# Splitting eight more pairs of products a third time, with the two partial results of one output block joined by DMA

## The chip, the cores and the metric

The kernel runs on one core of a Trainium2 chip. The metric is the device time of one execution in microseconds (us); lower is better. The core has TensorE (PE, matmuls), VectorE (DVE), ScalarE (ACT), GpSimd (POOL, here only an issuer of DMAs) and SyncE (SP, an issuer of DMAs), each with its own queue of instructions in order, and 16 DMA engines that serve the DMAs of all queues.

## The reference

A mixture of experts with soft routing: every token goes through all eight experts, weighted by its softmax.

```python
# x: 16 x 512 x 512, router_logits: 16 x 512 x 8, expert_weights: 8 x 512 x 2048, all float32
probs = softmax(router_logits)
for e in range(8):
    output += probs[:, :, e:e+1] * np.matmul(x, expert_weights[e])
```

It is one matmul of a left side of 8192 x 4096 (x times the probability of each expert, the experts side by side) with a right side of 4096 x 2048.

## The kernel before

**Outer level.** The matmul is cut with Winograd's form of Strassen's method: seven products in place of eight. The left side is cut into 16 row blocks q of 512 tokens, each into an even and an odd half of 256 tokens (`h = 2q` and `2q + 1`), and into experts 0 to 3 and 4 to 7. The weights are cut into four blocks B11, B12, B21, B22 of 2048 x 1024. For each q there are the products P1 (even rows, experts 0 to 3, with B11), P2 (even rows, experts 4 to 7, with B21), and P5, P6, P7, P4, P3 on sums of these, with weights that are sums of blocks (`T1 = B11 - B12`, `T2 = B22 + T1`, `T3 = B22 - B12`, `T4`). C11, the even rows and first half of the columns, is P1 + P2. P1 is also an addend of M1, from which other blocks of the output come, so its result is kept in DRAM (`kept`) in any case.

**Inner level.** Each product (`Product`) is again cut by the same method into seven inner products, the steps 1, 5, 6, 2, 7, 3, 4. A step is 8 matmuls of 128 x 128 by 128 x 512, so a product has 56. One step of one product is called a slot. The left operands (`Left`: z, its `s2`, its `i`) are made by VectorE, the weights' inner sums (`inner_sums`) too. After each step `post` evacuates PSUM: `post_alone` mostly on ScalarE, `post_on_base`, for a product that adds a base, mostly on VectorE.

**Third level.** In some stages (`thirds`) the inner products 1 and 5 of a pair of products are cut once more, with the pair's two row blocks as the row halves: `by_thirds` runs 14 groups of four matmuls of 256 columns in place of four steps of eight matmuls of 512 columns, with left sums from `Thirds.make` on VectorE and weights from `third_sums`.

**Stages.** A stage is a pair of products with 14 slots, 112 matmuls or, split, 136. The list `stages` is in order: 15 stages of P1 and P2 (numbers 0 to 14, of which q = 0 and 1 of P1 are done ahead of them without an inner level), then stage 15 (`k5`) with two P5, 16 with one P6, 17 to 30 with P6 and P5, 31 (`k7`) with P6 and P7, 32 to 46 with P4 and P7, 47 (`k3`) with P4 and P3, 48 to 54 with two P3, and 55 with the last P3. Before, stages 0 to 3 hold P1 in pairs, 4 to 9 a P2 and a P1, 10 to 14 P2 in pairs; stages 1 to 3 and 48 to 54 are split.

**Order of the work.** From the first stage on, each engine's instructions stay in the order in which the program makes them. `hooks` (`at(stage, slot, make)`) put loads and sums at a slot; VectorE's work goes through one queue (`later`, `slack`), which a clock in the program empties as time allows. Loads of x and of the probabilities start two stages ahead (`start_loads`), the left operands are made one stage ahead (`queue_lefts`). A block of x that was not read before is loaded and cast by a DMA of POOL (`xs`) and transposed by DMAs of SP, then stored for later uses. Outputs, `kept` and weights sums are stored by POOL's DMAs (`pool`), bases are fetched by SP's (`Base.fetch`), sums of weights are fetched again by ScalarE's (`fetch_w`). Pools bound what can be under way: 15 weight tiles w (1 MB each), 12 tiles h for results, 10 tiles for x and probabilities. `wedge` loads half of one block of B12 and of B22 and makes T3, T1 and T2 of it.

**What P1 and P2 do with each other.** For q of 9 to 14 the P2 of a stage adds the P1 result of the stage before, which is still on chip; for the others it fetches `kept` as a base:

```python
if q >= QK:
    base = products[1, q].o.__getitem__
else:
    base = bases[2, q] = Base(kept_rows(q))
p = Product(right[2], left, to_out(q, 0, 0), base)
```

Of the kernel before, what the change touches and what calls it, by code (L numbers as in the profile page):

```python
# [31 lines left out]
def kernel(  # L32
# [19 lines left out]
    NB = 512  # L52
    NH = EH // 2
    WARM = 10
    HQ = 256
# [50 lines left out]
    def tt(o, a, b, op):  # L106
        dve(nc.vector.tensor_tensor(out=o, in0=a, in1=b, op=op))  # L107
# [12 lines left out]
    def pool(o, i, **how):  # L120
        note(nc.gpsimd.dma_start(out=o, in_=i, **how))  # L121
# [257 lines left out]
    def later(cost, make, first=False):  # L379
        t = Task(cost, make)  # L380
        (queue.appendleft if first else queue.append)(t)
        return t
# [238 lines left out]
                tt(o[tn], q if p in (5, 3) else x, base, ADD)  # L621


    QK = 9
    KEPT_Z = 14
    ND = QK // 2

    def out_rows(q, odd, cols, tn):
        t, n = tn
# [2 lines left out]
    def to_out(q, odd, cols, **how):  # L632
        return lambda tn, o: pool(out_rows(q, odd, cols, tn), o, **how)
# [59 lines left out]
    def kept_rows(q):  # L693
        return lambda tn: kept[q][tn[1], ds(tn[0] * HP, HP), :]

    def product(r, q, **how):
        left, loads = left_of(r, q)
        lefts[r, q] = left
        p = None
        if r == 1:  # L700
            def sink(tn, o):
                pool(kept_rows(q)(tn), o)
            p = Product(right[1], left, sink)
        elif r == 2:
# [24 lines left out]
        p.loads = loads  # L729
        products[r, q] = p  # L730
        return p

    products = {}
    forget = lambda *hs: [xs.pop(h, None) for h in hs]


    def start_loads(stage):
# [120 lines left out]
    forget(*range(0, 2 * QK, 2))  # L858
    rest = [15] + list(range(QK))
    for i in range(0, QK + 1, 2):  # L860
        k = add(product(2, rest[i]), product(2, rest[i + 1]))
        for slot, tn in zip((8, 10, 12, 13), INNER):
            for q in rest[i:i + 2]:
                if q < QK:
                    fetch_at(k if tn == (1, 0) else k - 1, 3 if tn == (1, 0) else slot, bases[2, q], tn)
    xs.clear()
    k5 = add(product(5, 0), product(5, 1))
    add(product(6, 0))
# [37 lines left out]
    def wedge(kn, e):  # L906

        t = new_w()
        a, b = t[:, ds(0, C), :], t[:, ds(C, C), :]
        rows = ds(e * C, C)  # L910

        def casts():
            cast_w(12, kn, e, a)
            cast_w(22, kn, e, b)

        def send(what, u):
            pool(kept_w(what, kn)[:, rows, :], u)

        def t3():
            u = new_u().rearrange("p (c two) t -> p c (two t)", two=2)  # L920
            tt(u, b, a, SUB)
            send("t3", u)

        def t1():
            tt(a, b11[kn][:, rows, :], a, SUB)
            send("t1", a)

        def t2():
            tt(b, b, a, ADD)
            send("t2", b)  # L930
        return casts, [t3, t1, t2]

    def wedge_at(stage, slot, kn, e, then):
        made = []

        def begin():
            casts, made_ = wedge(kn, e)
            casts()
            made.extend(made_)

        def go_on():
            for make in made:
                later(1.22, make)
        at(stage, slot, begin)
        at(*then, go_on)

    b21, t1, t2, t3 = {}, {}, {}, {}

    def cast21(kn):
        b21[kn] = cast_block(21, kn)  # L950

    for i, kn in enumerate(((0, 0), (0, 1), (1, 1), (1, 0))):
        at((11 * i + 8) // 14, (11 * i + 8) % 14, lambda kn=kn: cast21(kn))
# [12 lines left out]
    for i, (kn, e) in enumerate((kn, e) for kn in ((0, 0), (1, 0), (1, 1)) for e in range(2)):  # L966
        wedge_at(ND + i, 2, kn, e, (ND + i, 11))
# [4 lines left out]
    ODD = 0, 1  # L972


    made = {}

    def cast_odd(q):
        made[q] = cast_block(q, ODD)

    def odd_t():  # L980

        def make1():
            t1[ODD] = made[11]
            tt(t1[ODD], made[11], made[12], SUB)

        def make3():
            tt(made[12], made[22], made[12], SUB)
            pool(kept_w("t3", ODD), made.pop(12))

        def make2():  # L990
            t2[ODD] = made[22]
            tt(t2[ODD], made[22], t1[ODD], ADD)
        for make in (make1, make3, make2):
            later(2.29, make)

    def odd_t4():
        def make():
# [14 lines left out]
        return one(4, b[1, 0], b[1, 0], b[1, 1])  # L1012

    last2 = k5 - 1
    for stage, slot, q in ((9, 9, 12), (10, 2, 11), (10, 9, 22), (last2, 8, 21)):
        at(stage, slot, lambda q=q: cast_odd(q))
    at(11, 6, odd_t)
    for i, kn in enumerate(((0, 0), (1, 1), (1, 0))):
        fetch_at_w(11 + (8 + 4 * i) // 14, (8 + 4 * i) % 14, t1, "t1", kn)
        fetch_at_w(last2, 2 + 2 * i, t2, "t2", kn)  # L1020
    sums_at(12, 8, 5, t1, (5, 6))
    sums_at(13, 2, 5, t1, (7, 4))
    sums_at(last2, 9, 6, t2, (5, 6))
    at(k5, 4, odd_t4)
    sums_at(k5, 5, 6, t2, (7, 4))
# [10 lines left out]
    def part_of(what, kn, chunks):  # L1036
        return kept_w(what, kn)[:, chunks, :]
# [27 lines left out]
    def cast_part(q):  # L1065
        def load(t, kn, j, chunks):
            k, n = kn
            pool(t, expert_weights[(q // 10 - 1) * HE + 2 * k + j // 2, ds(j % 2 * 2 * P, 2 * P),
                                   ds((q % 10 - 1) * NH + n * NB, NB)].rearrange("(c p) n -> p c n", p=P))
        return load  # L1070

    def load_part(what):
        def load(t, kn, j, chunks):
            pool(t, part_of(what, kn, chunks))
        return load
# [7 lines left out]
            pool(part_of("t4", kn, chunks), t)  # L1083
        later(0.69, make)

    def keep_raw(t, kn, chunks):
        pool(part_of("b22", kn, chunks), t)

    by_parts(k5 + 2, 4, 13, 7, load_part("t3"), None, (7,))
    by_parts(*slots_after(k5 + 2, 4, 56), 28, 4, load_p4, less_t2, (9, 20))  # L1090
    by_parts(k7 + 4, 4, 36, 3, cast_part(22), keep_raw, (9, 16))


    RAW = {1: (0, 0), 2: (1, 0), 3: (1, 1)}
# [30 lines left out]
        return load.begin  # L1125
    at(k3 - 1, 10, load_z(0))
    at(k3, 2, load_z(1))
    third3 = {}

    def third_of_p3(p):  # L1130
        def make():
            third3[p] = third_sums(right[3].w[p])
        later(2.76, make)
    at(k3, 3, lambda: third_of_p3(1))
    at(k3, 5, lambda: third_of_p3(5))
    wait_for[k3] = 6


    finish = products[3, 15]
    finish.base = Base(lambda tn: out_rows(15, 0, 1, tn))  # L1140
# [79 lines left out]
```

## Time and profile before

| | before |
|---|---|
| median of 3 runs | 1369.01 us (1368.84 to 1369.75) |
| profiled execution, first to last instruction (span) | 1367.0 us |
| PE busy | 1359.6 us (99%) |
| DVE busy | 1124.8 us (82%) |
| ACT busy | 207.3 us (15%) |
| POOL busy | 411.8 us (30%) |
| moved by DMA | 360.09 MB |

The profiled execution is known by its span; the runs lie 1.8 to 2.8 us above it, the median 2.0 us, for what lies around the first and last instruction. The rows in the text below are from that one execution. A row of a group gives busy time, mean ns of one, then the engine's idle time ahead of them and what ended it; a row of the timeline gives start, length, engine, line and operation, and in brackets the idle time ahead. A matmul's end is modelled, so rates are taken from starts. A line can be that of a helper: L107 is every VectorE tensor operation, L121 every DMA of POOL, L130 every matmul.

### The profile page before, as it was taken

The numbers are of one execution on the slowest core, as the hardware profiler recorded it, in microseconds if no ns is written. First come the engines' busy times: TensorE is split into PE (matmuls) and PEld (weight loads), VectorE is DVE, ScalarE is ACT, GpSimd is POOL, SyncE is SP. The second block draws the span as 40 slices with busy tenths as digits, with TensorE's granted clock in tenths as the row PEclk, the third lists the DMA queues.
The fourth block names the chain that finished last, engine by engine and source line by source line (L and its number), as shares of the span: only waits on it lengthen the run. The fifth ranks groups of instructions, "written<-read, shape, count | busy, mean of one in ns | idle before, by whom it ended". The sixth has DMA issues, their size and how long they took to land.

```text
span 1367.0 us, 18181 instructions
## 1 busy us (share of the span) xinstructions
PE 1359.6 (99%) x6630; PEld 645.4 (47%) x6630; DVE 1124.8 (82%) x1358; ACT 207.3 (15%) x397; POOL 411.8 (30%) x652
## 2 busy tenths in 40 slices
PE   9999999999999999999999999999999999999999
PEld 4555444444444444444444444444444444556554
DVE  7868767679789888788887888888889898898884
ACT  3232111100011111111111100000000000223331
POOL 3233233331223343333322112232332422233232
PEclk9999999999999999999999999999999999999999
DMA  9999999999899999999999998888897979999876
GB/s 185 207 246 233 229 254 255 244 294 385 252 309 273 334 343 317 292 277 316 309 302 324 322 399 240 199 237 208 231 265 203 259 184 298 328 306 240 189 122 127
DMA packets 193290, 360.09 MB, mean 263 GB/s; under 512 B 53168, under 2 KB 87216, under 8 KB 187696
## 3 DMA queue, kind: packets, MB, share of 16 engines
q0 software_dynamic: 88688, 185.12, 56.8%
q1 hardware_dynamic: 100480, 145.36, 35.4%
q10 hardware_dynamic: 4032, 28.44, 5.3%
q8 instruction: 52, 0.85, 0.3%
q14 instruction: 38, 0.31, 0.1%
HBM read 214.99 MB, written 171.11 MB: 282 GB/s over the span
## 4 chain that ended last, share of the span: by engine, by line
PE 97%; DMA 3%; POOL 0%; issue 0%; ACT 0%; DVE 0%; ACTq 0%; POOLq 0%; DVEq 0%
PE ps L130 71%; PE pt L130 25%; DMA h<-out_dram 2%; DMA w<-wd 1%; DMA w<-in_expert_weights_dram 1%; POOL w L121 0%; ACT h L614 0%; DVE ps L107 0%; ACT h L1168 0%; ACTq L164 0%; POOL ident L225 0%; POOLq L225 0%; DVEq L107 0%; POOLq L1204 0%
## 5 line engine op out<-in xcount | busy, mean ns | idle before, releaser
L130 PE MATMUL ps<-w,z 128*128 128x512 f16 (+1 forms) x3704 | 812.2, 376 | 0.8 <-DMA w<-wd 0.5
L130 PEld LDWEIGHTS <-z 128*128 128x128 f16 x5336 | 522.0, 98 | 606.2 <-issue 1.7
L121 POOL DMA_DIRECT2D out_dram<-h x380 | 248.8, 679 | 729.4 <-ACT h L614 337.0
L130 PE MATMUL pt<-w,z 128*128 128x512 f16 (+1 forms) x1632 | 357.7, 369 | 0.6 <-DMA w<-in_expert_weights_dram 0.5
L107 DVE TENSOR_TENSOR h<-ps,h 128x512 f32<-128x512 f32 x260 | 176.8, 686 | 120.9 <-PE ps L130 112.3
L107 DVE TENSOR_TENSOR z<-xT,pT 128x2048 f16<-128x2048 f16 x220 | 266.4, 1216 | 8.2 <-issue 7.2
L130 PE MATMUL ps<-w,d 128*128 128x512 f16 x880 | 199.1, 379 | 0.0
L107 DVE TENSOR_TENSOR h<-pt,h 128x512 f32<-128x512 f32 x155 | 105.7, 687 | 53.5 <-PE pt L130 46.7
L130 PEld LDWEIGHTS <-d 128*128 128x128 f16 x880 | 86.1, 98 | 101.7
L107 DVE TENSOR_TENSOR z<-z,d 128x2048 f16<-128x2048 f16 x110 | 132.4, 1215 | 0.0
L107 DVE TENSOR_TENSOR w<-w 128x1024 f16<-128x1024 f16 (+2 forms) x108 | 111.1, 1039 | 3.4 <-DMA w<-wd 1.7
L614 ACT COPY h<-ps 128x512 f32<-128x512 f32 x64 | 37.5, 586 | 486.2 <-PE ps L130 415.5
L601 ACT COPY h<-ps 128x512 f32<-128x512 f32 x90 | 52.7, 585 | 372.4 <-PE ps L130 316.0
L107 DVE TENSOR_TENSOR d<-z 128x1024 f16<-128x1024 f16 x110 | 74.6, 683 | 0.9
L107 DVE TENSOR_TENSOR ps<-ps,h 128x512 f32<-128x512 f32 (+1 forms) x86 | 54.0, 628 | 22.7 <-PE ps L130 18.6
L121 POOL DMA_DIRECT2D wd<-w x86 | 48.3, 585 | 41.6 <-DVE w L107 26.2
L121 POOL DMA_DIRECT2D w<-in_expert_weights_dram x65 | 48.9, 784 | 38.0 <-DMA wd<-w 28.1
L121 POOL DMA_DIRECT2D kept<-h x56 | 30.8, 550 | 60.2 <-DVE h L107 27.3
L597 ACT COPY h<-ps 128x512 f32<-128x512 f32 x65 | 36.7, 598 | 76.8 <-PE ps L130 67.3
L107 DVE TENSOR_TENSOR h<-h 128x512 f32<-128x512 f32 (+2 forms) x69 | 45.0, 674 | 0.6 <-ACT h L601 0.5
L107 DVE TENSOR_TENSOR z<-z,u 128x2048 f16<-128x2048 f16 x36 | 44.1, 1225 | 1.2
L107 DVE TENSOR_TENSOR u<-xT,pT 128x2048 f16<-128x2048 f16 x36 | 43.8, 1216 | 0.0
(72 smaller groups left out, 352.5 us busy)
## 6 DMA issues: line engine op xcount, KB each, us to landing
out_dram<-h POOLq DMA_DIRECT2D x380, 256.0 KB, 6.9
pT<-p_dram SPq DMA_DIRECT2D x126, 256.0 KB, 6.8
w<-wd ACTq DMA_DIRECT2D x27, 1024.0 KB, 9.7
h<-kept SPq DMA_DIRECT2D x100, 256.0 KB, 7.4
xT<-x SPq DMA_DIRECT2D x73, 256.0 KB, 6.7
wd<-w POOLq DMA_DIRECT2D x72, 256.0 KB, 7.5
w<-in_expert_weights_dram POOLq DMA_DIRECT2D x35, 512.0 KB, 10.5
h<-out_dram SPq DMA_DIRECT2D x68, 256.0 KB, 5.3
```

The source lines that it names most:

```text
L107: dve(nc.vector.tensor_tensor(out=o, in0=a, in1=b, op=op))
L121: note(nc.gpsimd.dma_start(out=o, in_=i, **how))
L130: note(nc.tensor.matmul(ps, z, w, start=start, stop=stop, skip_group_check=True))
L597: act(nc.scalar.copy(o[tn], q if p == 5 else x))
L601: act(nc.scalar.copy(o[TN[p]], b if p == 2 else x))
L614: act(nc.scalar.copy(o[tn], b))
```

## The change

P1 gets stages 0 to 6 in pairs, P2 stages 7 to 14 in pairs. Stages 1 to 5 and 8 to 13 are split a third time, where 1 to 3 were. P2 writes its result to the output without a base, and later 64 DMAs of POOL (`add_kept`), from DRAM to DRAM, add P1's kept result to it, 256 KB each: four per stage in stages 10 to 13, then one every five or six slots from stage 32 to 46, and four each in stages 49 and 50. T1 is no longer stored and fetched but made in place of B11 (`in_place`), all four blocks go through `wedge` (the block (0, 1) in stages 2 and 4, the others in stages 7 to 12), B22 is kept from there for the last P3 weights, and T2 is fetched in four blocks in stage 14. The third-level weights of P2 (`third2`) are made in stage 7. The diff, cut to its core:

```diff
-    ND = QK // 2
+    ND = 7
...
-            if q >= QK:
-                base = products[1, q].o.__getitem__
-            else:
-                base = bases[2, q] = Base(kept_rows(q))
-            p = Product(right[2], left, to_out(q, 0, 0), base)
+            p = Product(right[2], left, to_out(q, 0, 0))
...
-    for q in range(2, QK, 2):
+    for q in range(2, 16, 2):
         add(product(1, q), product(1, q + 1))
-    for q in range(QK, 15):
-        add(product(2, q), product(1, q + 1))
...
+    for q in range(0, 16, 2):
+        add(product(2, q), product(2, q + 1))
...
+        own = b11[kn][:, rows, :]
...
-        def t1():
-            tt(a, b11[kn][:, rows, :], a, SUB)
-            send("t1", a)
+        def in_place():
+            tt(own, own, a, SUB)
         def t2():
-            tt(b, b, a, ADD)
-            send("t2", b)
+            send("b22", b)
+            tt(a, b, own, ADD)
+            send("t2", a)
...
+    for kn, where in zip(((0, 0), (0, 1), (1, 1), (1, 0)), ((1, 8), (3, 2), (5, 0), (5, 9))):
+        at(*where, lambda kn=kn: cast21(kn))
...
+    for i, (kn, e) in enumerate((kn, e) for kn in (ODD, (0, 0), (1, 1), (1, 0)) for e in range(2)):
+        stage = ND + i - 2 if kn != ODD else 2 + 2 * i
+        wedge_at(stage, 2, kn, e, (stage, 11))
...
+    for i, kn in enumerate(ORDER):
         fetch_at_w(last2, 2 + 2 * i, t2, "t2", kn)
...
-    by_parts(k7 + 4, 4, 36, 3, cast_part(22), keep_raw, (9, 16))
+    by_parts(k7 + 4, 4, 36, 3, load_part("b22"), None, (9,))
...
+    third_at(ND, 5, third2, 2, 1)
+    third_at(ND, 7, third2, 2, 5)
...
+    def add_kept(q, n, t):
+        pool(out_f[ds(2 * q * HQ + t * HP, HP), ds(n * NB, NB)], kept[q][n, ds(t * HP, HP), :], accum_op=ADD)
+
+    for q in range(16):
+        for i in range(4):
+            where = (ND + 3, 14 * q + 3 * i) if q < 4 else (k7 + 1, 21 * (q - 4) + 5 * i) if q < 14 else (k3 + 2, 14 * (q - 14) + 3 * i)
+            at(*slots_after(where[0], 0, where[1]), lambda q=q, i=i: add_kept(q, i // 2, i % 2))
...
-    for stage in range(1, ND):
+    for stage in range(1, ND - 1):
         thirds[stage] = Thirds(*(p.left for p in stages[stage]), third)
+    for stage in range(ND + 1, last2):
+        thirds[stage] = Thirds(*(p.left for p in stages[stage]), third2)
```

More of the change, by code (lines that the diff above doesn't have):

```diff
@@ L621, in post_on_base @@
                 tt(o[tn], q if p in (5, 3) else x, base, ADD)
-    QK = 9
     KEPT_Z = 14
-    ND = QK // 2
+    ND = 7
     def out_rows(q, odd, cols, tn):
@@ L733 @@
     products = {}
-    forget = lambda *hs: [xs.pop(h, None) for h in hs]
     def start_loads(stage):
@@ L851, in fetch_at @@
             at(stage, slot, lambda tn=tn: base.fetch(tn))
-    for q in range(2, QK, 2):
+    for q in range(2, 16, 2):
         add(product(1, q), product(1, q + 1))
-    for q in range(QK, 15):
-        add(product(2, q), product(1, q + 1))
[L858 to L865, printed above, removed]
+    xs.clear()
+    for q in range(0, 16, 2):
+        add(product(2, q), product(2, q + 1))
     xs.clear()
@@ L922, in t3 @@
             send("t3", u)
-        def t1():
-            tt(a, b11[kn][:, rows, :], a, SUB)
-            send("t1", a)
+        def in_place():
+            tt(own, own, a, SUB)
         def t2():
-            tt(b, b, a, ADD)
-            send("t2", b)
-        return casts, [t3, t1, t2]
+            send("b22", b)
+            tt(a, b, own, ADD)
+            send("t2", a)
+        return casts, [t3, in_place, t2]
     def wedge_at(stage, slot, kn, e, then):
@@ L945, in wedge_at @@
         at(*then, go_on)
-    b21, t1, t2, t3 = {}, {}, {}, {}
+    b21, t2 = {}, {}
     def cast21(kn):
         b21[kn] = cast_block(21, kn)
-    for i, kn in enumerate(((0, 0), (0, 1), (1, 1), (1, 0))):
-        at((11 * i + 8) // 14, (11 * i + 8) % 14, lambda kn=kn: cast21(kn))
+    for kn, where in zip(((0, 0), (0, 1), (1, 1), (1, 0)), ((1, 8), (3, 2), (5, 0), (5, 9))):
+        at(*where, lambda kn=kn: cast21(kn))
     def sums_at(stage, slot, r, of, ps):
@@ L965 @@
     sums_at(ND - 1, 12, 2, b21, (4,))
-    for i, (kn, e) in enumerate((kn, e) for kn in ((0, 0), (1, 0), (1, 1)) for e in range(2)):
-        wedge_at(ND + i, 2, kn, e, (ND + i, 11))
+    ODD = 0, 1
+    for i, (kn, e) in enumerate((kn, e) for kn in (ODD, (0, 0), (1, 1), (1, 0)) for e in range(2)):
+        stage = ND + i - 2 if kn != ODD else 2 + 2 * i
+        wedge_at(stage, 2, kn, e, (stage, 11))
     def fetch_at_w(stage, slot, of, what, kn):
@@ L971 @@
     ORDER = ((0, 0), (0, 1), (1, 1), (1, 0))
-    ODD = 0, 1
     made = {}
@@ L978, in cast_odd @@
         made[q] = cast_block(q, ODD)
[L980 to L994, printed above, removed]
     def odd_t4():
@@ L1014 @@
     last2 = k5 - 1
[L1015 to L1019, printed above, removed]
+    at(last2, 8, lambda: cast_odd(21))
+    for i, kn in enumerate(ORDER):
         fetch_at_w(last2, 2 + 2 * i, t2, "t2", kn)
-    sums_at(12, 8, 5, t1, (5, 6))
-    sums_at(13, 2, 5, t1, (7, 4))
+    for stage, slot, p in ((last2 - 2, 8, 5), (last2 - 1, 2, 6), (last2 - 1, 8, 7), (last2, 1, 4)):
+        sums_at(stage, slot, 5, b11, (p,))
     sums_at(last2, 9, 6, t2, (5, 6))
@@ L1084, in less_t2 @@
         later(0.69, make)
-    def keep_raw(t, kn, chunks):
-        pool(part_of("b22", kn, chunks), t)
     by_parts(k5 + 2, 4, 13, 7, load_part("t3"), None, (7,))
     by_parts(*slots_after(k5 + 2, 4, 56), 28, 4, load_p4, less_t2, (9, 20))
-    by_parts(k7 + 4, 4, 36, 3, cast_part(22), keep_raw, (9, 16))
+    by_parts(k7 + 4, 4, 36, 3, load_part("b22"), None, (9,))
     RAW = {1: (0, 0), 2: (1, 0), 3: (1, 1)}
@@ L1127, with third_at @@
     at(k3, 2, load_z(1))
-    third3 = {}
-    def third_of_p3(p):
+    third2, third3 = {}, {}
+    def third_at(stage, slot, of, r, p):
         def make():
[L1132 to L1135, printed above, removed]
-    wait_for[k3] = 6
+            of[p] = third_sums(right[r].w[p])
+        at(stage, slot, lambda: later(2.76, make))
+    third_at(ND, 5, third2, 2, 1)
+    third_at(ND, 7, third2, 2, 5)
+    third_at(k3, 3, third3, 3, 1)
+    third_at(k3, 5, third3, 3, 5)
+    wait_for[k3] = 6
+    def add_kept(q, n, t):
[4 more added lines that the diff above has]
+            at(*slots_after(where[0], 0, where[1]), lambda q=q, i=i: add_kept(q, i // 2, i % 2))
     finish = products[3, 15]
```

## The prediction

> **What bounds the kernel now.** I read the page first (span, engines, clock, the chain that ended last), then busy time by stretches, with the stretches laid on stages, then TensorE's timeline at a stage's start, the DMA view of single stages, and last the chain of waits around the one place where TensorE stops.
>
> ```profile
> span 1367.0 us, 18181 instructions
> ...
> PE 1359.6 (99%) x6630; PEld 645.4 (47%) x6630; DVE 1124.8 (82%) x1358; ACT 207.3 (15%) x397; POOL 411.8 (30%) x652
> ...
> PEclk9999999999999999999999999999999999999999
> DMA  9999999999899999999999998888897979999876
> ...
> PE 97%; DMA 3%; POOL 0%; issue 0%; ACT 0%; DVE 0%; ACTq 0%; POOLq 0%; DVEq 0%
> ```
>
> TensorE carries 97% of the chain at the full clock, so time comes from the number of matmuls and from places where TensorE stops. VectorE is 82% busy and the DMA engines look full nearly everywhere: these two hand back what fewer matmuls gain. By stretches (stage bounds found by counting matmuls; x counts one neighbour too many on TensorE):
>
> ```profile
> core 0: us, PE busy (x) PEld busy (x) DVE busy (x) ACT busy (x) POOL busy (x), PEclk, DMA share, GB/s
> 200.00:600.00 400.00, 400.00 (x1855) 181.32 (x1853) 326.64 (x380) 47.24 (x81) 126.85 (x222) 1.00 1.02 299
> ...
> 64.48:87.94 23.46, 23.46 (x137) 13.30 (x136) 16.79 (x23) 8.46 (x18) 6.51 (x11) 1.00 1.26 239
> 87.94:111.32 23.38, 23.38 (x137) 13.31 (x136) 16.61 (x22) 8.40 (x18) 7.50 (x14) 1.00 1.21 225
> 255.57:279.74 24.17, 24.17 (x113) 10.98 (x112) 16.72 (x20) 3.50 (x6) 9.34 (x16) 1.00 1.10 250
> 799.47:824.78 25.31, 24.50 (x113) 10.87 (x112) 20.27 (x24) 1.17 (x2) 5.38 (x8) 1.00 1.04 389
> 824.78:848.95 24.17, 24.17 (x113) 10.95 (x112) 20.43 (x24) 1.17 (x2) 5.69 (x9) 1.00 0.87 237
> 1210.76:1234.40 23.64, 23.54 (x137) 13.29 (x136) 21.59 (x27) 8.23 (x18) 8.21 (x10) 1.00 1.07 275
> 1304.54:1327.92 23.38, 23.38 (x137) 13.31 (x136) 19.81 (x25) 8.23 (x18) 6.93 (x9) 1.00 0.69 90
> ```
>
> Stages of 112 matmuls take 24.17 us, split stages of 136 take 23.38 us (stages 2 and 53), and of the stages shown only stage 1 (+0.08), stage 32 (799.47, +1.14) and stage 49 (1210.76, +0.26) took longer. So a stage lasts as long as its matmuls, even at a DMA share of 1.26, until something is late by more than its lead.
>
> **The change, part by part.** A slot is one step of one product: 8 matmuls, 8 x 0.2157 = 1.73 us. *Eight more split pairs.* Before, stages 1 to 3 and 48 to 54 are split; after, stages 1 to 5 (P1), 8 to 13 (P2) and 48 to 54. The number of stages is the same. Each newly split pair swaps 32 matmuls of 512 columns for 56 of 256: 8 x 24 = 192 more matmuls, which the built program has. The split part of stage 1 begins and ends here:
>
> ```profile
> 64.48 1.04 PE L130 MATMUL pt<-w,z 128*128 128x256 f16 x8
> ...
> 70.59 1.67 PE L130 MATMUL ps<-w,d 128*128 128x512 f16 x7
> ```
>
> 56 matmuls in 70.59 - 64.48 = 6.11 us are 109.1 ns each. A 512-column one takes 400 / 1854 = 215.7 ns (one off for the edge). 32 x 215.7 = 6.90 us against 6.11 us is 0.79 us per pair, the same as 24.17 - 23.38. Eight pairs save **6.3 us**. [...]
>
> *VectorE's work.* The prices:
>
> ```profile
> L107 DVE TENSOR_TENSOR h<-z 128x1024 f16<-128x1024 f16 x6 | 4.1, 686 | 0.1
> L107 DVE TENSOR_TENSOR u<-w 128x2048 f16<-128x2048 f16 x6 | 7.3, 1215 | 0.0
> ```
>
> A split pair's own work is in the rows of stages 1 and 2: 16.6 to 16.8 us. P2 pairs become like P1 pairs, because they no longer add a base: their results are evacuated by ScalarE (8.4 us busy in a split stage, off the path). On top, stages 2, 4 and 7 to 12 each get a wedge (half of one of the four weight blocks: T3, T1 and T2 in three operations), 3 x 1.215 = 3.6 us. That makes 20.3 of 23.38 us; stage 49's row carries 21.59 and loses 0.26. The two blocks of third-level weights for P2 are 8 x 0.686 = 5.5 us in stage 7, not a split stage; its 27 operations, counted in the program, are 9 of 1.215 and 18 of 0.686 us, 23.3 of 24.17, and what is last in the queue is a wedge that nobody waits for. I take 0, with 0.3 per stage as the upper end.
>
> *Loads of P1 in pairs.* The pairs of stages 4 to 6 now need two raw x blocks each (before, one from stage 4 on), loaded two stages ahead by POOL's casting load and SP's transposes. Before, that was already close (the DMA view of 55 to 62 us, with the median time to land, and VectorE's timeline):
>
> ```profile
> xT<-xs SPq DMA_TRANSPOSE x4, 14.8
> ```
> ```profile
> 77.49 1.22 DVE L107 TENSOR_TENSOR z<-xT,pT 128x2048 f16<-128x2048 f16 x1 [4.44 <-issue]
> ...
> 83.75 0.68 DVE L107 TENSOR_TENSOR h<-ps,h 128x512 f32<-128x512 f32 x1
> ```
>
> Transposes issued there, beside B21's casting loads, took 14.8 us to land, and VectorE stood 4.44 us before a z (the row says "issue"; transposes issued up to 62 land up to 77, so I read them as the cause). The evacuation of step 7 then ran at 83.75 and ended at 84.43; the second product's step 4, whose bank it frees, starts about 2 x 1.73 us before the stage's end at 87.94, at 84.5. TensorE lost 0.08 us. So another 1 us of lateness is 1 us lost. After, the cast of one block starts at stage 1's slot 8 and two half blocks at the wedges in stages 2 and 4, so five stages come near this edge; bounds 0 and 5 x 1 us, and below 0 only the 0.08. I take 0.3, near the row, which got through.
>
> *What leaves the queues.* The fetches of P1's results into P2's bases go (36 from SP), T1's way through DRAM goes, and the last P3 weights are loaded and not cast. T2 is now fetched by ScalarE's queue in four blocks instead of three in stage 14, two slots apart, and the sum that needs the third is queued three slots (5.2 us) after it:
>
> ```profile
> w<-wd ACTq DMA_DIRECT2D x27, 1024.0 KB, 9.7
> ```
>
> So VectorE may stand 9.7 - 5.2 - 2.4 (the sum before it, 2 x 1.215) = 2.1 us there, and the evacuations behind it have two slots, 3.5 us: 0, with 1 as upper end.
>
> *The 64 added DMAs.* Each reads 256 KB of P1 from DRAM and adds it into 256 KB of the output. No such DMA is in the trace. The nearest are the accumulating stores of P3, alone in stage 53 (the DMA view of 1304.54 to 1327.92; columns packets, MB, share of 16 engines):
>
> ```profile
> q0 software_dynamic: 1150, 2.09, 68.7%
> ...
> out_dram<-h POOLq DMA_DIRECT2D x9, 256.0 KB, 6.8
> ```
>
> 0.687 x 23.38 = 16.1 us for eight of them (the ninth is cut by the edge): 2.0 us of all 16 engines each, 6.8 us to land. An addition from DRAM cannot write less than that, and its source read is one more DRAM access, so the upper bound is twice, 4 us. I take 2.0. In stages 10 to 13 four per stage (8 us) come where eight fetches went, at shares that row 255.57 shows to be harmless at 1.10. In stages 32 to 46 it is 2.7 per stage, 5.3 us or 0.22 of a stage: stage 33's 0.87 becomes 1.09, harmless by the same row. In stages 49 and 50, 1.07 becomes 1.41, beyond any row; but an output tile there is needed again seven slots (12 us) after its last store, against 6.8 to land: I take 0.2, upper end 3. Stage 32 is the place that pays. TensorE's timeline there, the chain of waits, and the DMA view of the stage:
>
> ```profile
> 821.32 7.08 PE L130 MATMUL ps<-w,z 128*128 128x512 f16 x32 [0.49 <-DMA w<-wd]
> ```
> ```profile
> 788.08 20.68 DMA h<-out_dram
> ...
> 809.26 12.02 DMA w<-wd
> ```
> ```profile
> q10 hardware_dynamic: 602, 4.31, 40.4%
> q1 hardware_dynamic: 1941, 3.53, 38.7%
> q0 software_dynamic: 693, 1.96, 24.2%
> ```
>
> A base fetch issued at 788.08 takes 20.7 us and the weights of P4's step 4 are issued behind it and take another 12.0 us; TensorE waits for them, the stage is 1.14 us long. The engines have no room here (sum 1.03 at 389 GB/s). After, additions start at slots 0 and 5 of this stage, before those weights land (a third at slot 10 comes behind them). Each adds up to 2.0 us in front of one link of that chain: bounds 0 (they fit into dips; not below, since nothing leaves this stage) and 4.0. I take 2.0, the middle, since no row is nearer to one end.
>
> **Sum.** -6.3 + 0.3 + 0.2 + 2.0 = -3.8 us. The span becomes 1367.0 - 3.8 = 1363.2; the median of the runs lies 2.0 us over the profiled span, so 1369.0 - 3.8 = **1365.2 us**.
>
> **The rivals.** (a) *The additions hide entirely*: stage 32's 1.14 us stays, nothing else appears, 1369.0 - 6.3 = 1362.7. For it: everywhere else a share over 1.0 cost nothing. Against: stage 32's chain has no lead left. 15%.
>
> (b) *P1's transposes come too late*, at the edge shown above: up to 1 us in each of five stages beyond the forecast, up to 1370.2, the middle 1367.7. For it: wedge casts now stand beside the transposes in stages 2 and 4. Against: two casts stood there in stages 0 to 2 too. 15%.
>
> (c) *Slower: POOL's queue blocks behind the additions.* In the built program every POOL DMA waits for the one eight before it. Stages 10 to 12 have 17 POOL DMAs each and 13 has 14, counted in the program: eight take at least 8 x 23.38 / 17 = 11.0 us. If an addition lands after more than that, the output stores behind it start late, and the 12 h tiles (a split stage without room of its own wants 14) come free late; ScalarE's copy of step 6 has four slots, 6.9 us, before step 7 needs its bank. The slowest 256 KB seen is the 20.7 us above: 20.7 - 11.0 - 6.9 = 2.8 us in each of four stages, 11.2 us, **1376.4**. It is slower than before by more than the bound from about (3.8 + 2.7) / 4 + 17.9 = 19.5 us of landing. For it, from the waits of ScalarE (total, times, longest):
>
> ```profile
> ACT h L601 <- DMA out_dram<-h: 56.4, 5, 17.3
> ```
>
> Output tiles do come free late at times. Against: accumulating stores land in 6.8 us. 18%.
>
> (d) *256 columns cost more than half of 512*, because a weight load no longer hides beside the shorter matmul:
>
> ```profile
> L130 PEld LDWEIGHTS <-z 128*128 128x128 f16 x5336 | 522.0, 98 | 606.2 <-issue 1.7
> ```
>
> From 6.90 / 56 = 123 ns per matmul on the split saves nothing. With a fifth of the 98 ns laid bare it would take 109 + 20 = 129 ns and cost 56 x 0.129 - 6.90 = 0.3 us per pair: 1369.0 + 2.6 + 2.5 = 1374.1. The rows say 109.1, all hidden. 1%. [...]
>
> (e) *The gain does not arrive*: the change does what it says, but the six P2 stages wait for VectorE as stage 49 does, 6 x 0.3 us, and stage 32 pays its upper end: -6.3 + 1.8 + 4.0 + 0.5 = 0, 1369.0. Against: the 20.3 us above are under stage 49's 21.59. 6%.
>
> **How the numbers follow.** The forecast has 45%. Its own spread is the bounds of stage 32: 1363.2 to 1367.2. This kernel's measurement tells about 0.2%, 2.7 us, from no change: the line lies at 1366.3. Faster: 15 from (a), 41 of the forecast's 45, 2 of (b) = 0.58. Same: 4 of the forecast, 12 of (b), 6 of (e) = 0.22. Slower: (c), (d) and 1 of (b) = 0.20. The range goes from just under (a), 1362.0 (half of stage 32's 1.14 gone too), over (b) and (e) to 1371.0, which is also the forecast with the additions' upper price (8.0 for stage 32 in place of 2.0, 1371.2); it leaves out (c) and (d).
>
> **What would show it.** Stages 4, 5 and 8 to 13 at 23.38 us each: the first term. Stage 32 at 26 to 29 us with its last matmuls waiting for w<-wd: the third. Additions landing in 7 to 10 us and a share of about 1.1 in stages 33 to 46: their price. Wrong would be: additions landing after 20 us, POOL waiting on its own DMAs in stages 10 to 13, a stage of 8 to 13 over 24.17 us, or VectorE standing more than 5 us before a z in stages 2 to 6.

## The result, and the profile after

The changed kernel takes 1373.82 us (median of 5 runs, 1372.35 to 1376.47) against 1369.01 us: 1.0038 times as long, interval 1.0026 to 1.0051. The forecast was 1365.2 us, with 1362.0 to 1371.0 as range. It is slower by 4.8 us, not faster by 3.8.

From the page of the changed kernel (span, busy time, DMA share by slices, POOL's queue, the chain that ended last, the added DMAs as a group of instructions, then as issues with their landing time):

```profile
span 1374.7 us, 18740 instructions
...
PE 1356.7 (99%) x6822; PEld 664.7 (48%) x6822; DVE 1125.2 (82%) x1369; ACT 263.5 (19%) x525; POOL 461.2 (34%) x707
...
DMA  9899997899999999999999999999998999999976
...
q0 software_dynamic: 93536, 199.80, 62.1%
...
PE 81%; DMA 15%; issue 2%; DVE 1%; POOL 1%; ACT 0%; DVEq 0%; POOLq 0%; ACTq 0%
...
L121 POOL DMA_DIRECT2D out_dram<-kept x64 | 61.4, 1002 | 17.9 <-DMA out_dram<-h 12.8
...
out_dram<-kept POOLq DMA_DIRECT2D x64, 256.0 KB, 9.7
```

VectorE's busy time is what it was, and TensorE's is 2.9 us less, yet the span is 7.7 us longer (1374.7 against 1367.0; this execution is the slowest of the five, so its losses are some 3 us larger than the median's). The chain says where to look: before, TensorE carried 97% of it, now 81%, and DMAs 15%. TensorE waits in a few places. By stretches, laid on the stages by counting matmuls (stages 4, 8, 6, 19, 20, 32, 33 and 51):

```profile
core 0: us, PE busy (x) PEld busy (x) DVE busy (x) ACT busy (x) POOL busy (x), PEclk, DMA share, GB/s
135.35:158.73 23.38, 23.38 (x137) 13.32 (x136) 15.96 (x21) 8.23 (x18) 7.98 (x14) 1.00 1.12 233
235.27:258.65 23.38, 23.38 (x137) 13.32 (x136) 18.51 (x24) 8.20 (x18) 7.54 (x14) 1.00 0.90 248
...
182.11:211.10 28.99, 26.02 (x113) 11.40 (x112) 18.50 (x16) 5.84 (x10) 4.32 (x8) 0.94 0.91 253
484.33:510.30 25.97, 24.34 (x113) 10.97 (x112) 19.10 (x25) 3.50 (x6) 9.07 (x17) 1.00 1.09 306
510.30:536.06 25.76, 24.33 (x113) 10.97 (x112) 21.46 (x29) 3.50 (x6) 10.36 (x20) 1.00 1.10 335
802.33:828.08 25.75, 24.51 (x114) 10.87 (x112) 20.52 (x24) 1.17 (x2) 8.10 (x11) 1.00 1.05 354
828.08:853.75 25.67, 24.34 (x114) 10.95 (x113) 20.09 (x24) 1.17 (x2) 7.73 (x12) 1.00 0.94 262
1262.31:1287.61 25.30, 23.70 (x137) 13.30 (x136) 20.64 (x26) 8.24 (x18) 10.92 (x14) 1.00 1.04 257
```

Against 24.17 (112 matmuls) and 23.38 (136), and against the same stages before, the account of this execution is:

| where | us |
|---|---|
| eight newly split stages (4, 5, 8 to 13), each exactly 23.38 | -6.3 |
| stage 6 | +4.8 |
| stages 19 and 20 | +3.4 |
| stages 31 to 33 (3.45 over; before 1.15) | +2.3 |
| stage 51 | +1.9 |
| stages 1 and 49 (0.08 and 0.26 over before, now 0) | -0.3 |
| last stage | +1.2 |
| ahead of the first stage | +0.7 |
| sum | +7.7 |

**Stage 6.** VectorE's timeline, then TensorE's, both of the changed kernel:

```profile
192.43 1.23 DVE L107 TENSOR_TENSOR z<-xT,pT 128x2048 f16<-128x2048 f16 x1 [10.56 <-DMA xT<-xs]
...
198.50 6.81 DVE L107 TENSOR_TENSOR w<-w 128x4096 f16<-128x4096 f16 x3
205.23 1.28 DVE L107 TENSOR_TENSOR h<-ps,h 128x512 f32<-128x512 f32 x2
```
```profile
199.38 3.62 PE L130 MATMUL pt<-w,z 128*128 128x512 f16 x16
205.96 6.38 PE L130 MATMUL ps<-w,z 128*128 128x512 f16 x21 [2.97 <-DVE h L107]
```

VectorE stands 10.56 us before a left operand of stage 7, the transposes of a raw x block not having landed. Behind it in the queue are the other left operands (6.1 us), then three weight sums of P2 (6.8 us), then the evacuation that TensorE needs: it runs at 205.23, and TensorE has stood 2.97 us. Why the transposes are late stands a stage earlier, in the DMA view of 155 to 168:

```profile
w<-in_expert_weights_dram POOLq DMA_DIRECT2D x2, 512.0 KB, 13.9
...
xs<-in_x_dram POOLq DMA_DIRECT2D x2, 256.0 KB, 15.6
```

Stage 7 is P2 of q = 0 and 1, whose x blocks no stage has read before (P1 of q = 0 and 1 is done ahead of them). So POOL loads two raw x blocks in stage 5, two stages ahead, right behind the casting loads of `cast21` at slot 0. The x blocks take 15.6 us to land, SP's transposes can only start then, at the end of the stage, and slot 9 puts another block of B21 beside them.

The other 1.85 us of stage 6 (28.99 - 24.17 - 2.97) are nearly all slow matmuls, and the PEclk column shows them: 0.94 over the stage. The 21 matmuls behind the stop take 6.38 us; at full speed 21 take 20 x 0.2157 + 0.38 (the length of the last) = 4.69 us, 1.69 less. The remaining 0.16 is how a stop is counted, from the modelled end of the matmul ahead of it.

**Stage 51.** The chain of waits ahead of it and the DMA view of stages 49 and 50 (1215.5 to 1262.3), where the last eight additions were put:

```profile
1220.44 18.93 DMA out_dram<-kept
1239.37 20.17 DMA out_dram<-h
...
1260.56 17.70 DMA out_dram<-h
...
1278.35 0.60 ACT h L597
```
```profile
out_dram<-h POOLq DMA_DIRECT2D x13, 256.0 KB, 19.1
out_dram<-kept POOLq DMA_DIRECT2D x7, 256.0 KB, 19.4
```

Before, the stores of the same two stages (the DMA view of 1210.8 to 1258):

```profile
out_dram<-h POOLq DMA_DIRECT2D x18, 256.0 KB, 7.9
```

All accumulating stores land in 19 us there, where they took 7.9 before (6.8 alone in stage 53). The DMA share of the two stages hardly rose, to 1.08 and 1.09, not to the forecast's 1.41: the added work shows in the time to land. The chain ahead of the stop goes through an addition, and POOL holds the later stores back until earlier DMAs of its own have landed (22 of its issues to the output waited 30.9 us over the whole span for stores of results to land). The result tiles h come free late, ScalarE's copy waits for one, TensorE for the copy.

### The profile page after: what moved, and what is told of

Read it like the earlier page. It is cut to its first block, busy times and chain, and to the rows that moved or that the text cites. A ratio compares the mean times of both kernels' runs of the same rounds, so it can differ in the third digit from the quotient of the medians.

```text
span 1374.7 us, 18740 instructions
## 1 busy us (share of the span) xinstructions
PE 1356.7 (99%) x6822; PEld 664.7 (48%) x6822; DVE 1125.2 (82%) x1369; ACT 263.5 (19%) x525; POOL 461.2 (34%) x707
## 4 chain that ended last, share of the span: by engine, by line
PE 81%; DMA 15%; issue 2%; DVE 1%; POOL 1%; ACT 0%; DVEq 0%; POOLq 0%; ACTq 0%
PE ps L130 62%; PE pt L130 19%; DMA out_dram<-h 5%; DMA w<-wd 3%; DMA xT<-x 2%; DMA wd<-w 1%; DMA out_dram<-kept 1%; DMA w<-in_expert_weights_dram 1%; DMA xs<-in_x_dram 1%; DMA pT<-p_dram 1%; DMA h<-out_dram 1%; DVE h L107 0%; POOL w L121 0%; DVE z L107 0%; POOL out_dram L121 0%
## 5 line engine op out<-in xcount | busy, mean ns | idle before, releaser
L130 PE MATMUL ps<-w,z 128*128 128x512 f16 (+1 forms) x3768 | 822.8, 375 | 10.0 <-DVE h L107 7.4
L130 PEld LDWEIGHTS <-z 128*128 128x128 f16 x5272 | 516.0, 98 | 592.1 <-issue 14.9
L121 POOL DMA_DIRECT2D out_dram<-h x380 | 253.7, 694 | 639.3 <-ACT h L614 202.5
L130 PE MATMUL pt<-w,z 128*128 128x512 f16 (+1 forms) x1504 | 317.7, 359 | 1.2 <-DMA w<-in_expert_weights_dram 0.8
L107 DVE TENSOR_TENSOR h<-ps,h 128x512 f32<-128x512 f32 x244 | 166.2, 687 | 107.3 <-PE ps L130 87.7
L601 ACT COPY h<-ps 128x512 f32<-128x512 f32 x122 | 71.5, 586 | 435.9 <-PE ps L130 353.3
L107 DVE TENSOR_TENSOR h<-pt,h 128x512 f32<-128x512 f32 x123 | 83.4, 685 | 35.3 <-PE pt L130 34.0
L614 ACT COPY h<-ps 128x512 f32<-128x512 f32 x48 | 28.1, 586 | 377.7 <-PE ps L130 327.0
L597 ACT COPY h<-ps 128x512 f32<-128x512 f32 x97 | 53.8, 603 | 81.5 <-PE ps L130 67.0
L121 POOL DMA_DIRECT2D out_dram<-kept x64 | 61.4, 1002 | 17.9 <-DMA out_dram<-h 12.8
L593 ACT COPY ps<-ps 128x512 f32<-128x512 f32 x61 | 34.8, 570 | 112.6 <-PE ps L130 70.2
L121 POOL DMA_DIRECT2D wd<-w x77 | 42.6, 555 | 35.4 <-DVE w L107 20.2
```

The source lines that it names most:

```text
L130: note(nc.tensor.matmul(ps, z, w, start=start, stop=stop, skip_group_check=True))
L593: act(nc.scalar.copy(self.banks["b"], x))
L597: act(nc.scalar.copy(o[tn], q if p == 5 else x))
L601: act(nc.scalar.copy(o[TN[p]], b if p == 2 else x))
L614: act(nc.scalar.copy(o[tn], b))
```

## The experiments

Each ran beside the kernel before on the same chip. Stage times are of each one's profiled execution. In most variants single runs lie 5 to 16 us apart (before: most within 3 us, but on the chip of runs 1 to 4 five of 27 took 1372.6 to 1380.8), so stages tell more than medians. Each loss of a stage is read from one execution.

**1. noadds: the additions left out** (C11 lacks P1).

```diff
-            at(*slots_after(where[0], 0, where[1]), lambda q=q, i=i: add_kept(q, i // 2, i % 2))
+            pass
```

> The 64 additions are left out, so C11 lacks P1; all else as in the changed kernel. Theory (three separate causes: late raw x blocks in stage 6, 4.8 us; the additions, in stages 31 to 33 and 51, some 3 us of the profiled run; waits of the parts of P7's weights in stages 19 and 20, 3.4 us): stages 31 to 33 lose about 1.1 us in all as before the change, stage 51 takes 23.38 us, stage 6 stays at 28 to 29 us; 3 us faster than the changed kernel, about 1371. Rival A (the additions' traffic is behind all of it): stages 6 and 19 and 20 lose nothing either, about 1363. Rival B (the additions cost nothing, the losses in 31 to 33 and 51 are something else): no change, 1373 to 1374.

1368.47 us (1363.58 to 1375.67, 12 runs), 0.9987 of before (0.9965 to 1.0009). Stage 6 still loses 3.58, so that has nothing to do with the additions; stages 31 to 33 lose 0.37 and stage 51 nothing. In the traces of all kernels here, stages 33 and 51 lose only in the four with additions in stages 32, 33, 49 and 50 (the changed kernel, order, casts and parts: 0.35 to 1.5 in stage 33, 1.9 to 3.1 in stage 51), so those losses are theirs. Stages 31 and 32 lose up to 0.8 and 3.3 also with no additions at all (order_noadds_1 to _3 below), so how much of their 1.95 in the changed kernel is the additions' is not shown. Stages 19 and 20 lose nothing here. Two pages give an addition's price. POOL's queue (packets, MB, share of 16 engines' span) was shown above for the changed kernel; here:

```profile
q0 software_dynamic: 84320, 183.02, 55.6%
```

0.621 x 1374.7 - 0.556 x 1363.6 = 95.5 us for 64: 1.5 us of all 16 engines each.

TensorE's stop in stage 6 was longer here, 3.41 us, but the matmuls behind it ran at full speed:

```profile
205.66 6.63 PE L130 MATMUL ps<-w,z 128*128 128x512 f16 x30 [3.41 <-DVE h L107]
```

30 matmuls in 6.63 us are 29 x 0.2157 + 0.38: full speed. So a stop of about 3 us (2.97 in the changed kernel, 3.41 here) may or may not be followed by slow ones; the last section has the clock at both.

**2. order: P2 of q = 2 and 3 first,** so that stage 7 takes x blocks that have long been transposed.

```diff
-    for q in range(0, 16, 2):
+    for q in (2, 4, 0, 6, 8, 10, 12, 14):
         add(product(2, q), product(2, q + 1))
```

> P2's pairs in the order (2,3), (4,5), (0,1), (6,7) and on, so that the two x blocks that nobody read before are loaded in stage 7 and not in stage 5, between two casting loads of B21. Theory: stage 6 takes 24.2 us, the time falls by 4 to 5 us to about 1369. Rival (stage 6 is held by VectorE's work, P2's weight sums and left operands in an unsplit stage): stage 6 stays at 28 to 29 us, 1373 to 1374.

1370.27 us (1367.34 to 1378.7, 12 runs), 1.0016 (1.0002 to 1.0031). Stage 6 takes 24.17. The raw loads now come two stages later, where no B21 load stands ahead of them (the DMA view of 205 to 216):

```profile
xs<-in_x_dram POOLq DMA_DIRECT2D x2, 256.0 KB, 5.0
xT<-xs SPq DMA_TRANSPOSE x3, 6.8
```

5.0 us in place of 15.6. Stages 31 to 33 (2.75 over) and 51 (2.58) still lose, and stage 5 takes 24.05 in place of 23.38.

**3. casts: B21 loaded earlier,** the other cure for stage 6.

```diff
-    ... ((1, 8), (3, 2), (5, 0), (5, 9))):
+    ... ((0, 8), (1, 8), (3, 2), (3, 12))):
```

> The order of the changed kernel, but the four casting loads of B21 stand in stages 0, 1, 3 and 3, none in stage 5. Theory (the raw x blocks of stage 7 land late because they queue with these loads): stage 6 takes 24.2 to 25 us, 4 to 5 us faster, about 1369, unless stage 1 or 3 now loses some. Rival (it is VectorE's own work): stage 6 stays at 28 to 29 us. Rival (raw blocks of P2(0) and P2(1) are late whatever stands beside them): stage 6 stays above 26 us.

1378.5 us (1374.53 to 1388.57, 6 runs), 1.0074 (1.0044 to 1.0103). Stage 6 is clean, but stages 4 and 5 lose 1.4 and 7.2. VectorE's timeline there:

```profile
164.51 1.23 DVE L107 TENSOR_TENSOR u<-w 128x2048 f16<-128x2048 f16 x1 [7.03 <-DMA w<-in_expert_weights_dram]
```

Stage 5 stops TensorE twice: for 3.45 us, when ScalarE waits for a result tile whose store to `kept` lands late (eight matmuls of 256 columns behind it took 1.70 us from start to start, ahead of it 0.88), and for 1.83 us behind VectorE, which stands 7.03 us before the wedge's own weights. With raw x pairs and a wedge on POOL's queue, these stages have no room for another casting load. The loss moves with the loads, which supports the cause found in 2, though here the longer stage 5 also gives the transposes for stage 7 more time.

**4. late: the additions moved out of stages 32, 33, 49 and 50,** to stages 34 to 46.

```diff
-    ... else (k7 + 1, 21 * (q - 4) + 5 * i) if q < 14 else (k3 + 2, 14 * (q - 14) + 3 * i)
+    ... else (k7 + 3, 15 * (q - 4) + 4 * i)
```

> The additions of q = 4 to 15 all between stages 34 and 46, some 3.7 per stage, none in stages 32, 33, 49 and 50. Theory: stages 31 to 33 lose about 1.1 us in all, stage 51 takes 23.38 us, stages 34 to 46 stay at 24.17; 2.5 to 3.5 us faster than the changed kernel, about 1371. Rival (the additions cost where they stand, by their number): the loss moves to stages 34 to 46, no change.

1374.23 us (1370.5 to 1376.44, 10 runs), 1.0033 (1.0019 to 1.0047). Stages 33 and 51 are clean, stages 31 and 32 lose 0.51 and 0.27, stage 20 1.59. But stage 46 loses 4.93: there the weights turn over to P3's, and the chain of waits shows a store landing late:

```profile
1139.17 16.08 DMA out_dram<-h
```

Stage 6, left as it was, lost 6.98, of which TensorE stood 4.85; behind that it ran at half clock (last section).

**5. order_noadds and order_mid.** The first is 2 without the additions (C11 lacks P1), what the change brings without them and without stage 6's loss. The second is 2 with the additions in stages 34 to 44, between the two turnovers:

```diff
+    ... else (k7 + 3, 12 * (q - 4) + 3 * i)
```

> P2's pairs in the order (2,3), (4,5), (0,1), and on, and the 64 additions left out (C11 lacks P1). Theory: with both causes gone only the gain of the eight split pairs is left: 6.3 us under the kernel before, about 1362.5, stage 6 at 24.2 us, stages 31 to 33 at most 0.5 us over, 51 at 23.4. Rival (the rest of the change, casts and wedges beside P1's raw blocks, still costs): over 1365, with stages 3 to 6 or 17 to 20 long.

> The same order of P2's pairs, and the additions of q = 4 to 15 all in stages 34 to 44, 4.4 per stage, away from the stages in which weights turn over (31 to 33, 46, 47) and from P3. Theory: stages 34 to 44 have room, all stay at 24.17 us, stages 32 and 33 lose at most 0.5 us, 46 and 51 nothing; 1363 to 1365, faster than both kernels. Rival (additions cost by their number wherever they stand): some stages of 34 to 44 lose, 1367 to 1370.

order_noadds: 1365.89 us (1361.51 to 1377.87, 12 runs), 0.9985 (0.9962 to 1.0009); its profiled span is 1360.7. order_mid: 1366.12 us (1362.12 to 1370.71, 12 runs), 0.9981 (0.9970 to 0.9993), span 1361.3; once more on another chip (order_mid_again) 1364.67 us (1363.69 to 1366.29, 7 runs), 0.9972 (0.9961 to 0.9982). By these ratios it is faster than both kernels; of 56 stages only 20 and 37 lose, 0.6 and 0.5. The DMA views of stages 34 to 44, order_mid first:

```profile
q0 software_dynamic: 19125, 43.53, 76.4%
...
out_dram<-h POOLq DMA_DIRECT2D x87, 256.0 KB, 8.8
out_dram<-kept POOLq DMA_DIRECT2D x48, 256.0 KB, 9.1
h<-out_dram SPq DMA_DIRECT2D x44, 256.0 KB, 9.3
```
```profile
q0 software_dynamic: 12328, 31.27, 50.2%
...
out_dram<-h POOLq DMA_DIRECT2D x89, 256.0 KB, 5.5
h<-out_dram SPq DMA_DIRECT2D x44, 256.0 KB, 5.1
```

Beside the additions, stores and fetches there land in about 9 us instead of 5 to 5.5, and TensorE feels it little. Only stage 37 does: it loses 0.5 to 2.4 us in five of the six traces with additions in these stages (not in order_mid_nosplit's) and nothing in any other.

> The kernel with reordered P2 pairs and additions in stages 34 to 44 once more, beside the one with the parts further apart. Theory: 1362 to 1371 again, median about 1366, and VectorE stands 2 to 4 us before sums in stage 20. Rival (the first median was the chip's): another median by over 2 us.

**6. order_mid_nosplit: order_mid with P1 and P2 split only where before was (stages 1 to 3).**

```diff
-    third_at(ND, 5, third2, 2, 1)
-    third_at(ND, 7, third2, 2, 5)
-    for stage in range(1, ND - 1):
+    for stage in range(1, 4):
-    for stage in range(ND + 1, last2):
-        thirds[stage] = Thirds(*(p.left for p in stages[stage]), third2)
```

> As the kernel with that order and those places of the additions, but the eight new pairs are not split (stages 1 to 3 and 48 to 54 alone are, and P2's third-level weights are not made). Theory: each of stages 4, 5 and 8 to 13 takes 24.17 in place of 23.38 us, 6.3 us slower than with the splits, about 1370. Rival (the longer stages give DMAs more time, so part of the losses goes): 3 to 5 us slower only.

1371.42 us (1368.09 to 1383.02, 12 runs), 1.0024 (1.0008 to 1.0041). That is 5.3 us over order_mid by medians and 7.4 by spans (1.5 of those in stage 20); its unsplit stages take 24.17. The split's 6.3 us are there.

**7. Stages 19 and 20.** P7's weights are summed there in parts. In the changed kernel the chain of waits runs through them, a store of one part, then POOL's issue and the load of the next, then VectorE's sum:

```profile
510.62 11.10 DMA wd<-w
...
522.28 0.55 POOL w L121
522.84 7.49 DMA w<-wd
...
530.54 0.70 DVE w L107
```

Two cures were tried: each part summed three slots later, so that its load has more time, in the changed kernel (parts) and in order_mid (order_mid_parts), and parts further apart (13 slots are 22.5 us, 18 are 31).

```diff
-    by_parts(k5 + 2, 4, 13, 7, load_part("t3"), None, (7,))
+    by_parts(k5 + 2, 4, 13, 7, load_part("t3"), None, (10,))    # parts
+    by_parts(k5 + 2, 4, 18, 7, load_part("t3"), None, (7,))     # order_mid_apart; order_mid_16: 16
-    by_parts(*slots_after(k5 + 2, 4, 56), 28, 4, load_p4, less_t2, (9, 20))
+    by_parts(*slots_after(k5 + 2, 4, 72), 28, 4, load_p4, less_t2, (9, 20))   # order_mid_apart
+    by_parts(*slots_after(k5 + 2, 4, 64), 25, 4, load_p4, less_t2, (8, 17))   # order_mid_16
```

> The changed kernel with one number changed: the sums of P7's weight parts (stages 17 to 20) are queued ten slots after their loads and not seven. Theory (VectorE stands up to 5.5 us before these sums in stages 19 and 20 with the evacuations queued behind, which TensorE feels only in some executions): stages 19 and 20 take 24.17 us in every profile, the median falls by 1 to 3 us to 1371 to 1373, the runs lie closer together. Rival (chance of that one profile, no part of the median): no change.

> The reordered P2 pairs and the additions in stages 34 to 44, with the sums of P7's weight parts ten slots after their loads. Theory (the waits in stages 19 and 20 are what spreads the runs from 1362 to 1371): most runs at 1362 to 1364, median about 1363. Rival (the spread has another place): median 1366 as without it.

parts: 1381.55 us (5 runs), 1.0099 (1.0085 to 1.0113), with 6.1 us lost in stage 21. order_mid_parts: 1370.13 us (12 runs), 1.0026 (1.0007 to 1.0045), with 2.1 and 1.8 us lost in stages 21 and 22. The theory that a load only needs more time fell. POOL's timeline in parts shows why:

```profile
503.50 2.13 POOL L121 DMA_DIRECT2D w<-wd  x4 [10.00 <-DMA wd<-w]
...
529.54 0.54 POOL L121 DMA_DIRECT2D w<-wd  x1 [9.35 <-DMA wd<-w]
```

A part's load goes into the tile that the part before is still being stored from. With the sum later its stores are later too, and the next load stands at the head of POOL's queue for 10 us, with output stores behind it.

> As the kernel with reordered P2 pairs and additions in stages 34 to 44; the four parts of P7's weights stand 18 slots apart and not 13, sums seven slots after the loads as at first, P4's parts 16 slots later. Theory (a part is loaded into the buffer that the part before stored from, so its loads wait for those stores: 12 us to the sums, 6 for them, 10 to land are more than 13 slots, 22.4 us, and less than 18, 31 us): VectorE waits under 1 us before these sums, stages 19 to 23 all take 24.17 us, most runs at 1361 to 1364, median about 1363. Rival (P4's parts now crowd stages 22 to 30 instead, or the spread has another place): median 1366 or more.

> The kernel with reordered P2 pairs and additions in stages 34 to 44, P7's weight parts 16 slots apart (27.6 us, against 28 us from load to landed stores) and P4's four parts 25 slots apart with their two steps at 8 and 17 slots, so that the last ends 4 slots earlier than at first and stays out of the turnover in stages 30 to 32. Theory: stages 19 to 22 and 31 to 32 all take at most 24.7 us, median about 1363, faster than any before. Rival (each move of the parts only shifts the loss along these full stages): 1365 to 1370, with the loss in some of stages 21 to 31.

order_mid_apart: 1371.49 us (12 runs), 1.0026 (1.0016 to 1.0037). Stages 19 to 22 lose nothing, as the theory of the shared buffer wants, but the last part of P4's weights now falls into the turnover, and stages 31 and 32 lose 8.7. order_mid_16: 1367.66 us (1363.51 to 1374.4, 12 runs), 0.9996 (0.9980 to 1.0011). Stages 19 to 22 and 31 are clean in its profile, the median is not better than order_mid's.

**8. What spreads the runs** (order_noadds_1 to _3: order_noadds again, one profiled execution each).

> The kernel of order_noadds once more (P1 is not added to C11), to see one of its longer executions in a profile: its runs lay in two groups, 1361.5 to 1363.7 and 1368 to 1378 us. [...] Rival: the excess is spread over many stages, under 1 us each, with no stop over 2 us and a clock of 1.000. A short execution (about 1362) decides nothing.

> As order_noadds_1, another execution. Theory: if it is over 1367, one or two stages of 19 to 22 hold 4 us or more; over 1372, also a mean clock under 0.999 with matmuls 427 ns apart behind a stop. Rival: the excess lies elsewhere, in the turnover of weights (stages 31 to 33) or over many stages.

> As order_noadds_1, a third execution of the same kernel: over 1367 us, theory a few us in one or two of stages 19 to 22, rival an excess elsewhere or spread; about 1362 decides nothing.

1366.50, 1363.22 and 1364.65 us; no long one among them. But one kernel lost time in three different ways: 1.46 us in stage 5, 1.83 in stage 20 and 0.52 in stage 31, with some 1.4 more ahead of the first stage, where the granted clock was 0.96 over the first 41 us; 0.78 and 0.51 in stages 31 and 32; 3.28 in stage 32 alone. So in these executions the excess is neither in stages 19 to 22 alone nor spread thinly: it is one or two stops of 1 to 3 us, in places where other traces of this study lose too, and which of them is late differs by execution. Of the six long runs of order_noadds, four had a mean clock of 0.996 to 0.999 (the longest two, 1375.49 and 1377.87 us, 0.998 and 0.996), which would fit stops with slow matmuls behind them; 1369.88 and 1371.32 us had 1.000. No profile of one was had, so what makes them long stays open.

## Why the prediction was wrong, point by point

- *Eight more split pairs, -6.3*: right. Every one takes 23.38 us in the changed kernel, stages 8 to 13 in every trace with the split, and order_mid_nosplit, whose unsplit stages take 24.17, confirms it. Stages 4 and 5 are nearer an edge: stage 5 takes 0.2 to 1.46 us longer in six other traces, and in casts both lose. Rival (d) did not occur: at 256 columns the weight loads stayed hidden, with 13.32 us of them in the 23.38 us of stage 4, in which TensorE was busy for all 23.38.
- *VectorE's work, 0*: right; no split stage of 8 to 13 is longer, so rival (e) as placed did not occur.
- *Loads of P1 in pairs, 0.3*: **the step that failed**, by 4.5 us. The mechanism was named (transposes late behind casting loads, VectorE before a z) and so was the sign that would show it wrong (over 5 us before a z in stages 2 to 6). But the price assumed that 1 us more of lateness is 1 us lost, spread over stages that each had the lead of stage 1. In fact the lateness was 10.56 us in one stage, since the two B21 loads at slots 0 and 9 of stage 5 and the two raw x blocks of stage 7's P2 meet on POOL's queue. The prediction looked at P1's pairs and not at the first P2 pair. And the queue behind the late operand counted: the other left operands and three weight sums, 6.1 and 6.8 us, stood between it and the evacuation. Rival (b) had the mechanism and the bound of 5 us over five stages; one stage nearly took it.
- *What leaves the queues, T2's fetch, 0*: right; stage 14 takes 24.17.
- *The additions.* Landing time 9.7 us, inside the forecast's 7 to 10; engine time 1.5 us each, under its 2.0. The share of about 1.1 that was foreseen for stages 33 to 46 did not come: 0.94 in stage 33. Stage 32 itself took 25.75 us, just under the 26 to 29 forecast, its last matmuls waiting for w<-wd as foreseen (0.86 us). The +2.0 became +2.3 in stages 31 to 33 (in order +1.6). That the size fits is in part luck: stage 32 lost 3.28 us in order_noadds_3, with no additions, so only stage 33's 1.5 is shown to be theirs, and the link through which it came there is another, a load of x:

```profile
804.32 24.45 DMA xT<-x
```

- *Stages 49 and 50, 0.2 (upper 3)*: mis-sized, 1.9 in this profile and 2.6 in order's. The 12 us until a tile is needed again were set against 6.8 us of a lone store; in these very stages it was 7.9 before, and beside additions 19.1.
- *Rival (c)*: not where it was put. In stages 10 to 13 the additions landed after less than the 19.5 us from which it decides, and no stage was longer (the DMA view of 282.03 to 375.55):

```profile
out_dram<-kept POOLq DMA_DIRECT2D x16, 256.0 KB, 11.6
```

  Its chain (stores land late, h tiles come free late, ScalarE waits, TensorE waits) is that of stage 51.
- *Not foreseen at all*: stages 19 and 20, 3.4 us in this profile. The additions do not stand there, and the diff does not touch those parts. The same stages lose 0 to 3.8 us in the variants (and 2.1 in order_mid_nosplit, without the added splits), so it is an edge that the reordered kernel sometimes goes over and that before did not in its profile. What in the change brings it to the edge was not found. The last stage's 1.2 us and the 0.7 ahead of the first were not explained either.

In sum the sign was lost by stage 6 (4.8 instead of 0.3) and the two unforeseen or mis-sized terms (stages 19 and 20, stage 51: 5.3 instead of 0.2). With stage 6 mended and the additions between the turnovers the kernel takes 1364.7 to 1366.1 us, about what had been forecast for the change as it stands; that is not the forecast's sum come true, which holds 2.0 us for stage 32 that these kernels do not pay there.

## What to carry to other kernels

Moving a step moves its neighbours' loads too: list what each queue carries in each stage after the move, and look first at the stage where two kinds of work meet for the first time (here the first P2 pair behind the last B21 loads). Price a late operand by the whole in-order queue behind it, not by its own lateness. Here added DMAs cost little where fetches had slack (in order_mid's stages 34 to 44, with 48 of them, only stage 37 lost, 0.5 us) and much where weights turned over (4.93 us in late's stage 46) or result tiles were short (1.9 us in the changed kernel's stage 51), so it was their place, more than their bytes, that decided.

## What the runs showed of the hardware

**A stop can cost more than itself, and its length alone does not decide.** TensorE's busy time and granted clock around stage 6's stop in the changed kernel, around the same stop in noadds, and around stage 46's in late:

```profile
203.54:206.95 3.41, 0.99 (x5) 0.48 (x5) 3.41 (x4) 0.00 (x0) 0.69 (x2) 1.00 0.01 4
206.95:210.36 3.41, 3.41 (x10) 1.22 (x8) 3.41 (x4) 0.59 (x1) 2.01 (x4) 0.50 0.82 300
210.37:213.78 3.41, 3.41 (x17) 1.56 (x16) 3.41 (x4) 1.16 (x2) 1.60 (x3) 1.00 0.37 144
```
```profile
200.83:204.25 3.42, 1.41 (x7) 0.54 (x6) 3.42 (x2) 0.00 (x0) 0.00 (x0) 1.00 0.60 232
204.25:207.66 3.41, 2.00 (x10) 0.94 (x10) 3.41 (x6) 0.08 (x1) 1.62 (x3) 1.00 0.21 76
```
```profile
1157.26:1160.66 3.40, 1.16 (x7) 0.41 (x5) 3.37 (x4) 0.00 (x0) 0.00 (x0) 1.00 1.07 264
1160.67:1164.08 3.41, 3.41 (x10) 1.17 (x9) 3.38 (x4) 0.00 (x0) 0.00 (x0) 0.50 1.04 417
```

After the stops of 2.97 us (stage 6 of the changed kernel) and 2.24 us (stage 46 of late) the granted clock was 0.50 for 3.41 us (in the changed kernel matmuls start 427 ns apart there, 216 ahead of the stop); during and after the stop of 3.41 us in noadds it stayed at 1.00. So in these traces a shorter stop was followed by slow matmuls and a longer one by none. What decides is not shown; no run was made to test it.

At half clock for 3.41 us, 1.7 us of work is lost, so stage 6's loss is 2.97 + 1.69 + 0.16. Stage 6 of late had a clock of 0.87 from 202 to 206 us, 0.50 from 206 to 210 and 0.78 from 210 to 214, which is half clock from 205.0 to 211.8 us, 4.0 us of it behind the stop: 4.85 + 2.0 of its 6.98.

**Adding from DRAM to DRAM** took POOL 1002 ns per issue against 694 for an output's store from SBUF, 1.5 us of the 16 engines per 256 KB, and 9 to 12 us to land, 19 where it stood among accumulating stores.
